# A transformer layer on one core: queries, keys and half the probabilities transposed by transfers, some low parts made by GpSimd, the head's loads placed anew

## The chip, the core and the metric

The kernel runs on one core of a Trainium2 chip. Time is the device time of one execution, in microseconds, as a median of several executions; the time before is 1294.08 us (three executions, 1293.95 to 1294.24). The profile is of one execution. Its engines are TensorE (PE, with PEld for its weight loads), VectorE (DVE), ScalarE (ACT), GpSimd (POOL) and SyncE (SP, which here only issues transfers).

## The reference, cut to what matters

One layer of a diffusion transformer is applied to two groups of 128 tokens: context ("prompt", s = 0 in the kernel) and latent ("sample", s = 1). Both use the same weights, all in float32.

```python
D_MODEL = 2048; HEAD_DIM = 128; A_HEADS = 8; A_KV_HEADS = 2; B_HEADS = 8; D_FF = 8192
def ada_mod(cvec, w_ada, b_ada):
    m = jax.nn.silu(cvec) @ w_ada + b_ada
    return jnp.split(m, 6, axis=-1)          # shift1, scale1, gate1, shift2, scale2, gate2
...
h = rms_norm(x, norm1_w) * (1 + sc1) + sh1
qa, ka, va, qb, kb, vb, ga, gb = project_heads(h, w_in, ...)    # one 2048 x 8704 product, then RMS norms on q and k
oa = window attention A (8 query heads, 2 key heads, a sink logit; rotary for latent tokens)
ob = neighbourhood attention B (8 heads, a position bias for latent tokens)
#    latent queries also see 128 cached context keys: two key blocks of 128; context queries see one block
ya = oa @ w_br_a;  yb = ob @ w_br_b
x = x + g1 * ((sigmoid(ga) * ya + sigmoid(gb) * yb) @ w_out)
h2 = rms_norm(x, norm2_w) * (1 + sc2) + sh2
x = x + g2 * (jnp.square(jax.nn.relu(h2 @ w_up)) @ w_down)
```

Beside the two token groups the outputs hold the context's keys and values.

## The kernel before, in words

**Products in three parts.** A float32 operand is split into a high part (rounded to the format that TensorE reads at full speed) and a low part, the rest. A product is three matmuls: high x high, low x high, high x low. Weights come from HBM as tiles of 128 partitions by 1024 columns (512 KB). ScalarE's copy writes the high part (`wH <- raw`, line 112), VectorE subtracts it to get the low part (`wL <- raw, wH`, line 277). For the weight tiles listed in `LO_DMA` the low part is made without VectorE: ScalarE writes minus the high part, and a transfer issued by GpSimd adds the weights to it from HBM (`minus_plus`).

**Steps.** The unit of the program's order is the step: one weight tile, 256 rows by 512 columns of a matrix, used for both token groups: 12 matmuls of 128 x 512. There are 456 steps: 0 to 71 for queries, keys and values, 72 to 135 for the gates, 136 to 167 for the two branches, 168 to 199 for `w_out`, 200 to 215 for the first up-projection columns, and from 216 on seven rounds of 16 steps of up-projection (`up_pair`, which forms two column blocks by fewer products of sums of weights, in the PSUM banks Q1 to Q7) and 16 of down-projection.

**What sets the order.** Each engine works through its instructions in the order in which the program issues them; `run()` walks over the steps and issues for each, in this order, loads that are due (`load_at`, table `RUN` says how far ahead), the high and low parts of coming steps (`prep_to`; `HIA` and `LOOK`), the step's matmuls, and the work hung on the step by `at(i, ...)` and `ex(i, ...)`. All places are tables of step numbers at the top of the file. Buffers come from fixed slots (table `SLOTS`): which slot each tile gets is written down, and a tile waits until its slot's last reader is done.

**The head.** The modulation for the first norm is made in two ways: pairs of 128-row blocks (`mod_pair`, eight loads `araw` of 512 KB and 64 small matmuls each, placed after the step in `ADA_AT`), and, for the last blocks, dot products by VectorE. `XS_AT` places the scaling of the activations.

**Dots.** The other modulation vectors (shift2, scale2, both gates) come from 288 instructions on VectorE, 128 rows x 1024 columns each: the transposed weights `aT` times the condition's row `cB`, summed along the row (line 1564). Both operands lie in SBUF; each load of `aT` serves two dots, one per token group. `DOTS1`, `DOTS` and `DOTS2` give the step of each load's pair.

**Attention.** `POST` gives the steps of the work on each of the seven query, key and value units `u`: `qk_stat` (sums of squares), `qk_apply` (norm and rotary), `qk_T`, in which TensorE transposes each head (128 x 128) into a PSUM bank `ps_qT`, from where ScalarE copies it out. `JOBS` gives the steps of eight attention jobs (mixer, token group s, half of the heads): scores, softmax, normalise, `probs_T` (TensorE transposes into `ps_PT`), values. Longer lists take another way, which the file has already and uses for the gates' merge and the MLP's activations: ScalarE writes two planes of 16-bit halves (`qk_planes`, `probs_planes`), SyncE's queue issues a transposing transfer (`qk_flip`, `probs_flip`), and ScalarE joins the halves again (`qk_join`, `probs_join`):

```python
fs = (qk_stat, qk_apply, qk_planes, qk_flip, qk_join) if len(ps) > 3 else (qk_stat, qk_apply, qk_T)
...
if flips:
    return scores, softmax, normalise, probs_planes, probs_flip, probs_join, values
return scores, softmax, normalise, probs_T, values
```

**PSUM** has eight banks of 128 x 512 float32: four accumulate the steps' products (`pacc`), four are for everything else (`paux`).

## Time and profile before

| | |
|---|---|
| median of three executions | 1294.08 us (1293.95 to 1294.24) |
| the profiled execution | 1294.03 us, of which the span of its instructions is 1291.9 us |
| DMA | 430.55 MB, 333 GB/s over the span |
| loads `raw <- in_w_in`, 512 KB each, issue to landing (median) | 9.9 us |
| accumulating transfers `wL <- in_w_down`, GpSimd's queue | 8.5 us |
| loads of the condition rows `cB <- silu` | 14, 512 KB each |

The page of the profile gives each engine's busy time as a share of the span, then the chain of work that ended last: followed back from the last instruction, it says on which engine the time lay that set the end. Rows of instruction groups read: line, engine, operation, output <- inputs, tile shape, count, then busy time and the mean length of one. A busy time of TensorE is modelled: matmuls overlap, so the distance between the starts of two instructions tells more than the length of one. Timeline rows begin with start and length in us.

### The profile page before, as it was taken

What the parts mean: (1) busy time and instruction counts of PE and PEld (TensorE: products, weight loads), DVE (VectorE), ACT (ScalarE), POOL (GpSimd) and SP (SyncE); (2) the same over time, 40 slices, a digit from 0 to 9 for tenths busy, and PEclk for the clock granted to TensorE, in tenths of its full rate; (3) what the DMA queues carried; (4) which work ended last, traced back from release to release, by engine and by line L of the source; (5) the groups of instructions that cost most, each with busy time, mean ns of one, the idle gap of its engine ahead of it and who ended that gap; (6) DMA issues with size and microseconds to landing.
All of it is one profiled execution on the core that took longest, in us unless ns stands there. A gap on an engine that the chain in (4) does not pass through costs nothing.

```text
span 1291.9 us, 18147 instructions
## 1 busy us (share of the span) xinstructions
PE 1281.9 (99%) x6082; PEld 1044.9 (81%) x6082; DVE 1209.6 (94%) x1611; ACT 960.6 (74%) x1363; POOL 105.9 (8%) x129
## 2 busy tenths in 40 slices
PE   8999999999999999999999999999999999999998
PEld 4777788888878888888887888888888888888887
DVE  4599999999999999999889999999999999999997
ACT  5535778888766765746798888888889887989871
POOL 0000002121200000001101000100000000010100
PEclk9999999999999999999999999999999999999999
DMA  9999999999999999998899999899898979979995
GB/s 377 418 420 418 380 385 387 329 351 327 369 360 354 385 383 330 364 392 259 265 279 329 295 329 307 273 350 313 272 355 249 321 267 311 344 231 361 385 341 166
DMA packets 158429, 430.55 MB, mean 333 GB/s; under 512 B 53072, under 2 KB 54336, under 8 KB 158336
## 3 DMA queue, kind: packets, MB, share of 16 engines
q1 hardware_dynamic: 145264, 383.39, 79.1%
q0 software_dynamic: 12880, 45.91, 16.6%
q8 instruction: 47, 0.77, 0.2%
q14 instruction: 46, 0.38, 0.1%
q10 hardware_dynamic: 192, 0.10, 0.1%
HBM read 403.35 MB, written 14.99 MB: 324 GB/s over the span
## 4 chain that ended last, share of the span: by engine, by line
PE 96%; DMA 3%; DVE 0%; ACT 0%; issue 0%; SPq 0%; ACTq 0%
PE acc L337 18%; PE acc L335 18%; PE acc L336 18%; PE Q L1338 7%; PE Q L1339 7%; PE Q L1337 7%; PE acc L466 5%; PE acc L468 5%; PE acc L467 5%; DMA raw<-in_w_in 2%; PE ps_ada L352 1%; PE ps_S L853 1%; DMA araw<-in_w_pair 1%; PE acc L1144 1%; PE acc L1143 1%; PE acc L1142 1%
## 5 line engine op out<-in xcount | busy, mean ns | idle before, releaser
L112 ACT ACTIVATE wH<-raw 128x1024 fp32r<-128x1024 f32 (+1 forms) x347 | 344.6, 1042 | 65.5 <-DMA raw<-in_w_in 18.6
L277 DVE TENSOR_TENSOR wL<-raw,wH 128x1024 fp32r<-128x1024 f32 x297 | 347.4, 1217 | 5.2 <-ACT wH L112 4.8
L1564 DVE CUSTOM_DVE_ANT_0 junk<-aT,cB,cols 128x1024 uint8<-128x1024 f32 x144 | 178.8, 1285 | 0.0
L466 PE MATMUL acc<-wH,hH 128*128 128x512 f32 x276 | 108.5, 393 | 0.0
L468 PE MATMUL acc<-wH,hL 128*128 128x512 f32 x276 | 107.5, 389 | 0.0
L467 PE MATMUL acc<-wL,hH 128*128 128x512 f32 x276 | 107.5, 389 | 0.0
L335 PE MATMUL acc<-wH,hH 128*128 128x512 f32 x256 | 102.9, 402 | 0.0
L337 PE MATMUL acc<-wH,hL 128*128 128x512 f32 x256 | 99.9, 390 | 0.0
L336 PE MATMUL acc<-wL,hH 128*128 128x512 f32 x256 | 99.8, 390 | 0.0
L1564 DVE CUSTOM_DVE_ANT_0 junk<-aT,cB,gc_g 128x1024 uint8<-128x1024 f32 x64 | 79.3, 1279 | 0.0
L112 ACT ACTIVATE uH<-raw 128x1024 fp32r<-128x1024 f32 x56 | 58.9, 1051 | 17.3 <-DVE raw L1409 15.4
L1415 DVE TENSOR_TENSOR tL<-t,tH 128x1024 fp32r<-128x1024 f32 x56 | 68.2, 1218 | 2.0 <-ACT tH L112 1.9
L1415 DVE TENSOR_TENSOR uL<-raw,uH 128x1024 fp32r<-128x1024 f32 x56 | 68.2, 1217 | 0.2
L1403 DVE TENSOR_TENSOR t<-raw 128x1024 f32<-128x1024 f32 x56 | 68.1, 1217 | 0.0
L112 ACT ACTIVATE tH<-t 128x1024 fp32r<-128x1024 f32 x56 | 58.7, 1049 | 9.5 <-DVE t L1403 7.3
L466 PEld LDWEIGHTS acc<-wH,hH 128*128 128x128 f32 x276 | 51.8, 188 | 12.5 <-issue 2.1
L468 PEld LDWEIGHTS acc<-wH,hL 128*128 128x128 f32 x276 | 51.8, 188 | 10.8
L467 PEld LDWEIGHTS acc<-wL,hH 128*128 128x128 f32 x276 | 51.9, 188 | 10.6
L112 ACT ACTIVATE XH<-raw 128x1024 fp32r<-128x1024 f32 x56 | 58.6, 1047 | 0.5 <-PE Q L1338 0.5
L337 PEld LDWEIGHTS acc<-wH,hL 128*128 128x128 f32 x256 | 48.0, 188 | 10.2
L335 PEld LDWEIGHTS acc<-wH,hH 128*128 128x128 f32 x256 | 48.1, 188 | 10.0 <-issue 0.7
L336 PEld LDWEIGHTS acc<-wL,hH 128*128 128x128 f32 x256 | 48.2, 188 | 9.9 <-issue 0.7
(673 smaller groups left out, 3389.4 us busy)
## 6 DMA issues: line engine op xcount, KB each, us to landing
raw<-in_w_in SPq DMA_DIRECT2D x133, 512.0 KB, 9.9
raw<-in_w_down SPq DMA_DIRECT2D x128, 512.0 KB, 9.3
raw<-in_w_upF SPq DMA_DIRECT2D x112, 512.0 KB, 6.3
aT<-in_w_adaT SPq DMA_DIRECT2D x80, 512.0 KB, 9.8
aT<-in_w_gT SPq DMA_DIRECT2D x64, 512.0 KB, 9.9
araw<-in_w_pair SPq DMA_DIRECT2D x48, 512.0 KB, 9.9
raw<-in_w_out SPq DMA_DIRECT2D x32, 512.0 KB, 9.7
XL<-in_w_upF POOLq DMA_DIRECT2D x21, 512.0 KB, 8.1
```

The lines of the kernel that those rows point to most:

```text
L112: act.activation(out, in_, AF.Copy)
L277: dve.tensor_tensor(st["lo"], st["raw"], st["hi"].bitcast(F32), op=OP.subtract)
L335: pe.matmul(acc[tb], sh, wh[:, k, :], start=f, stop=False, **kw)
L336: pe.matmul(acc[tb], sh, wl[:, k, :], start=False, stop=False, **kw)
L337: pe.matmul(acc[tb], sl, wh[:, k, :], start=False, stop=l, **kw)
L466: pe.matmul(acc[tb], sh, wh[:, k, :], start=kt == 0 and k == 0 and not held and not seeded, stop=False, **kw)
L467: pe.matmul(acc[tb], sh, wl[:, k, :], start=False, stop=False, **kw)
L468: pe.matmul(acc[tb], sl, wh[:, k, :], start=False, stop=last and k == 1 and not hold, **kw)
L1337: pe.matmul(acc, stat[0], hi, start=f, stop=False)
L1338: pe.matmul(acc, stat[0], lo, start=False, stop=False)
L1415: dve.tensor_tensor(b[n + "L"], v, b[n + "H"].bitcast(F32), op=OP.subtract)
L1564: dve.tensor_tensor_reduce(out, box["raw"], cB[s, tag], 1.0, dst if second else baT[:, part, fb:fb + 1], OP.mult, OP.add, dst)
```

## The change

- **Transposes.** All seven lists of `POST` get five entries, and the four jobs on latent tokens (s = 1, two key blocks) seven: their transposes go by planes, transposing transfer and join. The four jobs on context tokens keep TensorE's. For query units of mixer A the join also applies the scale that the copy out of PSUM applied.
- **PSUM.** `paux` has two banks instead of four; a new pool `pwide` holds one tile of two banks, used in turn by the modulation of the very first blocks, by a copy of a condition row (`cW`), and by the banks Q4 and Q3 of `up_pair`. The product Q3 of a round's last block moves ahead in the order, so that Q5 ends last.
- **Dots.** ScalarE copies a condition row into the two-bank PSUM tile (`cond_up`, as many steps ahead of the dots as the table `CW` says), and dots read it there, except the 42 pairs listed in `BUF`, which read SBUF as before. Dots are grouped two loads at a time (`dot_runs`): two dots with one row, then two with the other.
- **Low parts by GpSimd.** `POOL_LO` names for 79 such pairs of dots a step whose low part GpSimd is to subtract at the same time (`lo_pool`), if it has none by then; VectorE writes one column of it just before, which orders the slot's reuse.
- **Tables.** `LO_DMA` falls from 65 entries to 39. The second to sixth modulation pairs, the scalings, the constants, the dots and the sums of the MLP get new steps; `HIA`, `LOOK`, `RUN` and `SLOTS` are new throughout.

```diff
-DOTS1 = [16, 17, 17, 19, 21, 27, 28, 32, 33, 34, 34, 38, 38, 38, 40, 40]
+DOTS1 = [15, 22, 24, 25, 29, 30, 31, 33, 34, 35, 36, 38, 40, 40, 42, 42]
...
-LO_DMA = [54, 64, 77, 81, 90, 96, 98, 104, 106, 107, 113, 115, 125, 126, 134, 137, 147, 154, 167, 179, 193, 195, 197, 199, 202, 203, 215, 216, 220, 222, 224, 226, 228, 230, 235, 242, 248, 252, 271, 277, 280, 294, 297, 302, 312, 316, 328, 335, 340, 346, 354, 356, 370, 382, 386, 390, 393, 397, 403, 408, 418, 434, 438, 448, 449]
+LO_DMA = [79, 130, 169, 182, 186, 199, 210, 220, 222, 230, 239, 241, 248, 252, 254, 279, 286, 290, 311, 312, 324, 342, 352, 354, 356, 362, 374, 378, 382, 386, 390, 403, 406, 407, 414, 418, 422, 436, 451]
...
-ADA_AT = [None, 5, 13, 20, 24, 38]
-XS_AT = {1: 14, 2: 2, 3: 23}
-POST = {('kvA', 0): [54, 57, 78], ('qA', 0): [54, 59, 66], ('qA', 1): [62, 70, 79], ('kB', 0): [71, 71, 79], ('qB', 0): [75, 82, 91], ('kB', 1): [89, 101, 104], ('qB', 1): [82, 87, 106]}
-JOBS = [[81, 85, 87, 93, 102], [82, 84, 88, 97, 111], [80, 86, 97, 103, 112], [88, 98, 103, 109, 111], [103, 103, 106, 115, 122], [105, 105, 108, 109, 126], [108, 108, 119, 123, 126], [113, 114, 117, 121, 125]]
+ADA_AT = [None, 4, 10, 19, 24, 39]
+XS_AT = {1: 0, 2: 10, 3: 26}
+POST = {('kvA', 0): [56, 58, 72, 75, 76], ('qA', 0): [52, 58, 68, 69, 74], ('qA', 1): [57, 65, 70, 83, 83], ('kB', 0): [74, 77, 81, 85, 90], ('qB', 0): [70, 73, 90, 93, 95], ('kB', 1): [80, 95, 105, 106, 109], ('qB', 1): [80, 83, 88, 93, 95]}
+JOBS = [[80, 81, 86, 102, 113], [86, 87, 97, 99, 102, 103, 108], [90, 90, 92, 108, 125], [95, 96, 104, 107, 113, 113, 118], [100, 100, 115, 119, 123], [106, 106, 109, 114, 120, 124, 128], [115, 115, 119, 123, 125], [117, 117, 119, 122, 124, 126, 128]]
...
+RN = 2
+BUF = [0, 2, 9, 12, 15, 16, 21, 24, 29, 31, 32, 34, 38, 40, 45, 47, 50, 52, 55, 60, 62, 65, 66, 69, 71, 73, 76, 82, 84, 94, 97, 100, 102, 104, 108, 117, 123, 127, 133, 135, 139, 143]
...
+POOL_LO = {43: 89, 44: 94, 46: 95, 48: 100, 49: 101, 51: 102, 57: 109, 58: 110, 59: 111, 61: 112, 88: 153, 116: 246, 118: 269, 119: 272, 120: 276, 122: 278, 124: 307, 125: 308, 128: 334, 129: 337, 130: 336, 141: 402, 53: 103, 68: 125, 86: 150, 41: 88, 126: 310, 89: 152, 4: 31, 132: 346, 72: 128, 87: 157, 54: 106, 121: 277, 90: 154, 93: 158, 134: 369, 80: 136, 96: 168, 138: 376, 91: 155, 8: 39, 98: 171, 22: 58, 14: 45, 33: 80, 115: 247, 81: 144, 77: 133, 5: 35, 64: 119, 3: 30, 136: 371, 83: 143, 19: 55, 42: 92, 7: 42, 109: 185, 28: 70, 137: 373, 10: 41, 111: 196, 27: 68, 103: 172, 70: 126, 107: 195, 23: 61, 67: 120, 79: 139, 142: 404, 101: 173, 99: 170, 114: 242, 105: 184, 17: 50, 110: 183, 78: 132, 92: 162, 36: 82}
...
-    paux = ctx.enter_context(tc.tile_pool(name="paux", bufs=4, space=bass.MemoryType.PSUM))
+    paux = ctx.enter_context(tc.tile_pool(name="paux", bufs=2, space=bass.MemoryType.PSUM))
+    pwide = ctx.enter_context(tc.tile_pool(name="pwide", bufs=1, space=bass.MemoryType.PSUM))
...
+    def lo_pool(st):
+        if "lo" in st or "hl" in st:
+            return
+        pool_hi(st)
...
+        st["lo"] = G("wL", F32R)
+        pool_minus(st["lo"], st["raw"], st["hi"])
+
+    def pool_minus(lo, full, hi):
+        dve.tensor_copy(lo[:, 0:1], hi.bitcast(F32)[:, 0:1])
+        pool.tensor_tensor(lo, full, hi.bitcast(F32), op=OP.subtract)
...
-        for s, w in enumerate({"qB": (2, 2), "kB": (None, 3)}.get(u[0], ())):
+        for s, w in enumerate({"qA": (0, None), "qB": (2, 2), "kB": (None, 3)}.get(u[0], ())):
...
-            for name in ("Q3", "Q4", "Q5") + (("Z",) if len(fast) < 8 else ()):
+            box["Q4"], box["Q3"] = pair("Q43")
+            for name in ("Q5",) + (("Z",) if len(fast) < 8 else ()):
...
-                    todo.append(("Q3", sc(j, 3), b["XH"][:, hi], b["XL"][:, hi]))
+                    todo.insert(4 if end else 5, ("Q3", sc(j, 3), b["XH"][:, hi], b["XL"][:, hi]))
...
+    def cond_up(s, q, tag):
+        cW[0] = wide("cW")
+        copy(cW[0], cB[s, tag])
+
+    def dots_of(k, run_, s, q, tag):
+        if k in POOL_LO:
+            lo_pool(wsteps[POOL_LO[k]])
+        for box, job, later in run_:
+            dot(box, job, later, s, cB[s, tag] if k in BUF else cW[0])
+        if k + 1 in POOL_LO:
+            pool_hi(wsteps[POOL_LO[k + 1]])
```

Three places show what the tables move. The first is TensorE's order at the end of the first units, where `ps_qT` receives the transposed heads of `u_qA` and `u_kB`; before:

```order
L335 MATMUL acc<-wH,hH_1663 128x512
L336 MATMUL acc<-wL,hH_1663 128x512
L337 MATMUL acc<-wH,hL_1664 128x512
L782 MATMUL ps_qT<-ident,u_qA_1862 128x128 x8
L782 MATMUL ps_qT<-ident,u_kB_2233 128x128 x8
L335 MATMUL acc<-wH,hH_244 128x512
L336 MATMUL acc<-wL,hH_244 128x512
```

and after, at the same place:

```order
L374 MATMUL acc<-wL,hH_1733 128x512
L375 MATMUL acc<-wH,hL_1734 128x512
L373 MATMUL acc<-wH,hH_246 128x512
L374 MATMUL acc<-wL,hH_246 128x512
L375 MATMUL acc<-wH,hL_247 128x512
```

The matmuls of one unit's last step are followed directly by those of the next unit's first, with no transposes between.

The second is SyncE's order of loads in the head (`raw` weights of the steps, `araw` the modulation pairs, `cB` the condition rows, `aT` weights for dots); before:

```order
L531 DMA raw<-in_w_in 128x512 x3
L243 DMA raw<-in_w_in 128x1024 x6
L344 DMA araw<-in_w_pair 128x1024 x8
L243 DMA raw<-in_w_in 128x1024 x7
L1545 DMA cB_442<-silu 128x1024
L1545 DMA cB_444<-silu 128x1024
L243 DMA raw<-in_w_in 128x1024
L344 DMA araw<-in_w_pair 128x1024 x8
```

and after:

```order
L569 DMA raw<-in_w_in 128x512 x3
L256 DMA raw<-in_w_in 128x1024 x5
L382 DMA araw<-in_w_pair 128x1024 x8
L256 DMA raw<-in_w_in 128x1024 x6
L382 DMA araw<-in_w_pair 128x1024 x8
L256 DMA raw<-in_w_in 128x1024
L1593 DMA cB_423<-silu 128x1024
L1593 DMA cB_425<-silu 128x1024
```

Five weight loads instead of six stand ahead of the second modulation pair, and the third pair stands ahead of the condition rows instead of behind them.

The third is VectorE's order in the stretch of the dots beside attention (`cB` a condition row in SBUF, `cW` its copy in PSUM); before:

```order
L1564 ISA junk,shT_159<-aT,cB_1210,cols 128x1024
L1564 ISA shT_159 128x1
L277 TENSOR_TENSOR wL<-raw,wH 128x1024 x2
L1564 ISA junk,shT_159<-aT,cB_1212,cols 128x1024
L1564 ISA shT_159 128x1
L277 TENSOR_TENSOR wL<-raw,wH 128x1024
```

and after:

```order
L1612 ISA junk,shT_162<-aT,cW,cols 128x1024
L1612 ISA shT_162 128x1
L1612 ISA junk,scT_163<-aT,cW,cols 128x1024
L1612 ISA scT_163 128x1
L330 CAST wL<-wH 128x1
L1612 ISA junk,shT_162<-aT,cW,cols 128x1024
L1612 ISA shT_162 128x1
L1612 ISA junk,scT_163<-aT,cW,cols 128x1024
L1612 ISA scT_163 128x1
L290 TENSOR_TENSOR wL<-raw,wH 128x1024
```

Two dots of one row now stand together, they read `cW`, and a one-column cast stands ahead of a pair beside which GpSimd makes a low part.

More of the change, by code (lines that the diff above doesn't have):

```diff
@@ L106, in SM, with wide, pair @@
         return slot(sp, "s", [P, 8], F32, name)[:, :n]
+    def wide(name):
+        return pwide.tile([P, 1024], F32, name=name, tag="w")
+    def pair(name):
+        t = wide(name)
+        return t[:, 0:512], t[:, 512:1024]
     def bank(name, pool_=None):
@@ L348, in pair_mm_q @@
         if j == 0 and q == 0:
-            box["ps"] = bank("ps_ada")
+            box["ps"], box["sel"] = pair("ps_ada") if alone else (bank("ps_ada"), None)
         raw = box.pop((fb, q)).rearrange("p (k n) -> p k n", k=4)
@@ L390, in first_cols @@
         shT, scT = mod[0]
-        ps = bank("ps_sel")
+        ps = box.pop("sel")
         for i in (1, 0):
@@ L1551, in dot_load, with dot @@
         sync.dma_start(box["raw"], src)
-    def dot(box, job, second, s, tag):
+    def dot(box, job, second, s, row):
         which, fb = job
@@ L1563, in dot @@
         out = sp.tile([P, 1024], mybir.dt.uint8, name="junk", tag="J", bufs=2)
-        dve.tensor_tensor_reduce(out, box["raw"], cB[s, tag], 1.0, dst if second else baT[:, part, fb:fb + 1],
+        dve.tensor_tensor_reduce(out, box["raw"], row, 1.0, dst if second else baT[:, part, fb:fb + 1],
                                  OP.mult, OP.add, dst)
@@ L1617, in dots2 @@
+    def dots2():
+        order = [(("g2", fb), q, q) for q in range(2) for fb in range(KC)]
+        at_, n0 = list(DOTS2), 0
+        for r, n in enumerate(RUNS2):
+            dot_runs(at_[n0:n0 + n], order[n0:n0 + n], ("g", r), 2)
+            n0 += n
         for n in range(4):
-            i = DOTS2[(15, 15, 23, 31)[n]] + ROW_AT[n]
+            i = DOTS2[31] + ROW_AT[n]
             while wsteps[i]["key"][0] != "down":
```

121 lines of the change are left out of this document (74 added, 47 removed).

## The prediction

> **What bounds the kernel now.** I read the page first (busy times, the chain of waits by engine), then the chain in order of time, then timelines of single places.
>
> ```profile
> span 1291.9 us, 18147 instructions
> PE 1281.9 (99%) x6082; PEld 1044.9 (81%) x6082; DVE 1209.6 (94%) x1611; ACT 960.6 (74%) x1363; POOL 105.9 (8%) x129
> PEclk9999999999999999999999999999999999999999
> PE 96%; DMA 3%; DVE 0%; ACT 0%; issue 0%; SPq 0%; ACTq 0%
> ```
>
> TensorE's work is the time: 96% of the chain that ended last lies on it, at the full granted clock, and the 3% of DMA lie in the head. A busy TensorE alone would prove little, since matmuls overlap; the chain decides. So an instruction taken off TensorE is worth its pitch, and any other engine's work is worth nothing until it makes TensorE wait. VectorE, at 94%, is the nearest to that. The sum below is made on the profiled execution, 1294.03 us, of which 1291.9 are the span; the runs' median is 1294.08, so nothing is to be converted.
>
> **1. Transposes leave TensorE.** The trace has 52 transposes of queries and keys and 48 of probabilities:
>
> ```profile
> L782 PE MATMUL ps_qT<-ident,u_qA x16: 270/272/273, 226.7 to 264.2; 128*128 128x128 f32 x16
> L782 PE MATMUL ps_qT<-ident,u_kB x16: 272/272/273, 264.3 to 344.0; 128*128 128x128 f32 x16
> L782 PE MATMUL ps_qT<-ident,u_qB x16: 270/272/273, 303.3 to 352.1; 128*128 128x128 f32 x16
> L782 PE MATMUL ps_qT<-ident,u_kvA x4: 270/272/273, 260.2 to 260.5; 128*128 128x128 f32 x4
> L900 PE MATMUL ps_PT<-ident,prob x48: 270/272/273, 309.6 to 409.9; 128*128 128x128 f32 x48
> ...
> 262.97 0.39 PE L336 MATMUL acc<-wL,hH 128*128 128x512 f32 x1
> 263.20 0.40 PE L337 MATMUL acc<-wH,hL 128*128 128x512 f32 x1
> 263.44 1.04 PE L782 MATMUL ps_qT<-ident,u_qA 128*128 128x128 f32 x8
> 264.31 1.04 PE L782 MATMUL ps_qT<-ident,u_kB 128*128 128x128 f32 x8
> 265.10 0.48 PE L335 MATMUL acc<-wH,hH 128*128 128x512 f32 x1
> 265.42 0.40 PE L336 MATMUL acc<-wL,hH 128*128 128x512 f32 x1
> ```
>
> All 52 go, and the 32 of the four jobs with two key blocks; 16 stay. One lasts 272 ns, but they overlap: from 263.44 to 265.42 stand 16 transposes and one matmul (0.23 us, from 262.97 to 263.20), so 16 cost 1.98 - 0.23 = 1.75 us, or 0.109 us each, with the change-over included. 84 x 0.109 = **-9.2 us**. Nothing else leaves or joins TensorE.
> The Trainium skill (TensorE: Matmul & The Clock Gate, Part 4: PE-mode transpose) gives about 275 ns for a transpose in a kernel's context; by that the term would be -23 us. The trace shows that length too, 272 ns, but as a length that overlaps its neighbour's, and the row decides.
>
> **2. The head.** The loads of the second modulation pair now stand one load earlier in SyncE's queue, and TensorE takes the pair one step earlier (after step 4, not 5).
>
> ```profile
> 20.93 2.17 SPq L243 DMA_DIRECT2D raw<-in_w_in  x3
> 23.40 8.46 SPq L344 DMA_DIRECT2D araw<-in_w_pair  x8
> 32.82 7.78 SPq L243 DMA_DIRECT2D raw<-in_w_in  x7
> ...
> 38.12 3.23 PE L352 MATMUL ps_ada<-araw,early 128*32 128x256 f32 x56
> 42.06 0.64 PE L352 MATMUL ps_ada<-araw,early 128*32 128x256 f32 x8 [0.71 <-DMA araw<-in_w_pair]
> 42.63 0.50 PE L466 MATMUL acc<-wH,hH 128*128 128x512 f32 x1
> ```
>
> Eight issues take 9.42 us, 1.18 each: the queue moves at the pace of the transfers. The pair's last transfer now lands 1.2 us sooner, so TensorE leaves the pair at 41.4 instead of 42.63; but step 5 (12 matmuls x 0.23 = 2.7 us) then still lies ahead of it, where before it was done: **+1.5 us**. Ends: 0, if the queue is quicker there, and +2.7, if the pair's last load gains nothing. The later pairs move by as much in the loads as in the steps and have no stall in the chain, so they cost nothing.
>
> **3. Low parts by GpSimd beside dots that read PSUM.** The table holds 79, but 15 of its steps already have a low part when their turn comes: in the program's order GpSimd makes 64. VectorE loses 38 subtractions and gains 64 one-column casts; 27 accumulating transfers and ScalarE's 26 negations for them go; ScalarE gains 40 copies of the condition rows into PSUM. No row shows a GpSimd subtraction of 128x1024.
>
> ```profile
> 286.69 0.69 DVE L872 TENSOR_REDUCE mx<-ps_S 128x4 f32<-128x512 f32 x1
> 286.85 0.56 POOL L717 TENSOR_SCALAR_AFFINE_SELECT bias<-bias 64x384 f32<-64x384 f32 x1
> ...
> 335.06 1.28 DVE L1564 CUSTOM_DVE_ANT_0 junk<-aT,cB,cols 128x1024 uint8<-128x1024 f32 x1
> 336.26 1.56 DVE L1564 CUSTOM_DVE_ANT_0 junk<-aT,cB,cols 128x1024 uint8<-128x1024 f32 x1
> 336.82 1.42 POOL L719 TENSOR_SCALAR_AFFINE_SELECT bias<-bias 64x384 f32<-64x384 f32 x1
> ...
> L187 POOL TENSOR_TENSOR early<-early 32x128 f32<-32x128 f32 x1 | 0.4, 448 | 7.8 <-ACT early L186 7.8
> ...
> 195.50 3.49 DVE L277 TENSOR_TENSOR wL<-raw,wH 128x1024 fp32r<-128x1024 f32 x3
> 198.91 1.28 DVE L1564 CUSTOM_DVE_ANT_0 junk<-aT,cB,cols 128x1024 uint8<-128x1024 f32 x1
> ...
> L1109 DVE TENSOR_TENSOR t<-g,acc 128x512 f32<-128x512 f32 x15 | 10.2, 680 | 3.9 <-PE acc L1272 2.9 <-PE acc L1144 0.6 <-PE acc L337 0.4
> L1110 DVE TENSOR_TENSOR x<-x,t 128x512 f32<-128x512 f32 x8 | 5.5, 692 | 0.3
> ```
>
> These rows show a collision: the select takes 0.56 us beside a reduction that reads PSUM, and 1.42 beside a dot with both operands in SBUF, and that dot 1.56 instead of 1.28. A dot that reads PSUM should leave GpSimd alone, and should last as long as now (680 against 692 ns where one operand is PSUM). Two dots cover 2 x 1.20 = 2.4 us (335.06 to 336.26). GpSimd's subtraction lies between 0.56 x 1024/384 = 1.5 us (one input) and 8 x 0.448 = 3.6 us (two inputs, small, fixed cost counted eight times); I take the middle, 2.5. It overruns the two dots by 0.2 us at most, which VectorE pays only where a two-operand subtraction follows. VectorE: -38 x 1.14 (195.50 to 198.91 for three) + 64 x 0.1 = -37 us, with 64 x 0.2 = 13 of overrun still -24. It is not on the chain, so this buys little: the one place where TensorE waits for it after the head is
>
> ```profile
> 704.19 0.50 PE L1337 MATMUL Q<-uH,h22H 128*128 128x512 f32 x1
> 705.45 0.50 PE L1338 MATMUL Q<-uL,h22H 128*128 128x512 f32 x1 [0.76 <-DVE uL L1415]
> ```
>
> where 1.26 - 0.23 = 1.0 us is to be had; I take half, **-0.5**, between 0 and -1.0.
> The Trainium skill (SBUF — State Buffer, Who interferes with whom) says that a VectorE instruction with two SBUF inputs and a GpSimd instruction that reads SBUF lock each other out for the whole instruction, and not with one SBUF input; the 1.56 and 1.42 agree. The skill (GPSIMD Engine Reference, Performance versus the Vector engine) gives 4497 ns for a subtraction's like of 2048 elements; half of it, an estimate, is 2.2 us, inside the dots' cover.
>
> **4. What the transfers cost elsewhere.** In place of TensorE's transposes, ScalarE writes planes of half-words, SyncE's queue transposes them, and ScalarE joins them.
>
> ```profile
> 215.00:415.00 200.00, 200.00 (x975) 166.38 (x974) 197.05 (x304) 154.39 (x360) 31.59 (x29) 1.00 0.99 350
> ...
> L112 ACT ACTIVATE fTa<-pTa 128x1024 uint16<-128x1024 uint16 x32 | 41.9, 1362 | 7.6 <-DMA pTa<-pla 7.6
> L112 ACT ACTIVATE pla<-up 128x1024 uint16<-128x1024 uint16 x32 | 32.5, 1047 | 1.2 <-PE acc L336 0.7 <-PE acc L337 0.3
> L112 ACT ACTIVATE acc<-dsum 128x512 f32<-128x512 f32 x44 | 24.9, 591 | 5.6 <-DVE t L1109 3.0 <-DVE dsum L1491 2.6
> L283 ACT ACTIVATE wL<-wH 128x1024 fp32r<-128x1024 f32 x44 | 46.5, 1060 | 1.0
> ...
> ACT fTm L112 <- DMA pTm<-plm: 12.0, 3, 6.2
> ...
> ACT fTa L112 <- DMA pTa<-pla: 7.6, 2, 7.3
> ```
>
> From 215 to 415 us (window view: after the pair of times, busy PE, PEld, VectorE 197.05, ScalarE 154.39, GpSimd) ScalarE gets: 12 planes at 1.05 and 18 short ones at 0.6 (23 us), 21 half joins at 1.36 (29), 8 scalings at 0.6 (5), 8 copies into PSUM at 2 x 0.59 (9), and loses 12 negations at 1.06, 8 probability and 14 query and key evacuations at 0.6 (26 in all). Net +40, so 194 of 200 us. TensorE has its next high parts several steps (of 2.7 us) ahead, which covers short waits at the joins. I take **+0.5 us**, between 0 and +8 (three steps of delay).
> The transfers' own load balances: 11 transposes come, 14 accumulating transfers of that stretch go.
>
> **Sum:** 1294.0 - 9.2 + 1.5 - 0.5 + 0.5 = **1286.3 us**, 0.6% less. Its own terms' ends give 1284 to 1295.
>
> **Rivals.**
> *ScalarE waits for the transfers (slower).* Place: the joins between 215 and 415 us. All three transposes of the merged rows waited, 12.0 us in all, 4.0 each; of the MLP's activations' transposes only two did (7.6). Against it: most joins stand some steps behind their transfer. For it: the first join of one query tile stands at its transfer's own step, and ScalarE has 6 us of slack where VectorE had 3. At 4.0 each, 11 waits are 44 us: 194 + 44 - 200 = 38 late, of which some 7 steps of work ahead, 19 us, hide half: 1286.3 + 19 = **1305**. It decides from 25 us of waiting (2.3 per join), and makes the kernel slower than before from 33 (3.0).
> *GpSimd collides with VectorE (slower).* If its subtraction takes 3.6 us, it overruns the dots by 1.2; the 64 casts and overruns then cost 64 x 1.3 = 83 us against 43 saved, most of it in the stretch that had 3 us of VectorE free: there 20 low parts x 1.3 - 8 x 1.14 = 17 us over, less 3: 1286.3 + 14 = **1300**. It decides from 2.4 + 0.4 us a piece.
> *The order also heals the head.* If the new places cost nothing there and the 1.0 us is won whole: 1294.0 - 10.2 - 1.4 (the stall of 42.06 and the 0.71 before it) = **1282**.
> *The transposes were hidden anyway:* 1294. Against it: TensorE issues matmuls right before and behind them, with no gap.
>
> **Chances.** Forecast 0.70, ScalarE's waits 0.12, the collision 0.10, the healed head 0.05, hidden 0.03. The likeliest gives **1286.3**. The range is 1282 to 1297: below it 0.05, above it the full sizes of the two slower rivals, 0.13. What this measurement can't tell from no change is 0.2%, 2.6 us. The forecast and the healed head, 0.75, and 0.02 of half-sized rivals are faster: 0.77. Half-sized rivals and the hidden case are the same: 0.10. Slower: 0.13.
>
> **What would show it.** Right: 84 transposes fewer at an unchanged pitch of 0.109; dots on the PSUM rows at about 1.28 us; GpSimd's subtraction at 2 to 2.8 us; TensorE leaving the second pair near 41.4 with step 5 still to come; ScalarE at 95% or more from 215 to 400 us. Wrong: TensorE waiting for high parts behind joins, or for low parts while GpSimd runs; dots or subtractions of VectorE stretched beside GpSimd.

## The result and the profile after

The changed kernel takes 1309.82 us (median of four executions, 1307.53 to 1312.74) against 1294.06 (1293.95 to 1294.24). That is 1.0123 times the time before, with an interval of 1.0100 to 1.0145: slower by 15.8 us, where 1286.3 had been forecast. The profiled execution took 1307.53 us, of which 1305.8 are the span.

The page of the changed kernel has this, in the places of the rows shown of before; in the last two rows the number behind the busy time is the mean of one in ns:

```profile
span 1305.8 us, 18166 instructions
PE 1279.1 (98%) x5998; PEld 1038.2 (80%) x5998; DVE 1172.3 (90%) x1637; ACT 1009.9 (77%) x1404; POOL 231.4 (18%) x167
PEclk9999999999999899999999999999999999999999
PE 58%; DMA 5%; DVE 5%; ACT 3%; issue 3%; POOL 0%; DVEq 0%; SPq 0%; ACTq 0%; POOLq 0%
...
L331 POOL TENSOR_TENSOR wL<-raw,wH 128x1024 fp32r<-128x1024 f32 x62 | 149.3, 2408 | 546.5 <-DVE wL L330 287.2
L1612 DVE CUSTOM_DVE_ANT_0 junk<-aT,cW,cols 128x1024 uint8<-128x1024 f32 x102 | 126.1, 1273 | 2.5 <-ACT cW L125 2.5
```

Read alone, the first rows say that the change worked. There are 84 matmuls fewer, VectorE lost the 37 us that were forecast, GpSimd's subtraction takes 2.41 us and a dot on the PSUM rows 1.27. The chain is less help than before. Read back from the last instruction it reaches only to 337.23 us, where it lies on VectorE, so its 58% for TensorE can't be set beside the 96% of before; the kernel without one transfer that is shown below has 62% and is not slower than the one before. But the longest pieces of the chain are now transfers far behind the head, and one slice of the granted clock is an 8.

Where the time went is best seen from the starts of the steps' matmuls of 128 x 512 (those that write `acc` and `Q`), of which both kernels have the same number, 5298. The k-th of one is set beside the k-th of the other (us from the span's start):

```
  k      before    after    difference   since the row above
  300    107.51    107.98     +0.47         +0.47     (the head)
  900    249.33    248.91     -0.42         -0.89
 1400    387.83    375.87    -11.96        -11.54
 1500    412.81    404.30     -8.51         +3.45     (transposes gone)
 1600    439.97    442.56     +2.59        +11.10     <- here
 2100    554.36    558.26     +3.90         +1.31
 2800    718.55    725.68     +7.13         +3.23
 3100    786.69    795.14     +8.45         +1.32
 3500    877.41    890.29    +12.88         +4.43
 5200   1263.24   1277.27    +14.03         +1.15
```

Up to 404 us nearly all went as forecast. Then 11.1 us are lost between two rows, and some 11 more in small pieces behind. Of the 11.1, 1.1 are lost in the same place by the kernel without the transfer that is to blame: at the row of 1500 the changed kernel still has two matmuls of the values ahead (`ps_o` of `u_kvA`, 407.02 to 407.88 us) that the kernel before has behind it:

```profile
407.02 1.02 PE L962 MATMUL ps_o<-probT,u_kvA 128*128 128x512 f32 x2
407.88 1.05 PE L966 MATMUL ps_o<-probT,u_vB 128*128 128x128 f32 x8
```

The waits of TensorE in the changed kernel from 300 us on (the waiting and the releasing instruction; us in total, times, the longest) and the windows of that place (columns as in the window view of before):

```profile
PE ps_o L966 <- ACT probT L125: 8.0, 1, 8.0
PE Q L1376 <- DVE tL L1462: 5.1, 3, 3.2
PE acc L373 <- ACT up L125: 1.4, 1, 1.4
PE Q L1376 <- DMA XL<-in_w_upF: 0.8, 2, 0.4
```

```profile
215.00:415.00 200.00, 199.59 (x931) 164.32 (x930) 193.72 (x310) 186.03 (x370) 59.93 (x35) 1.00 1.04 346
418.00:427.00 9.00, 1.03 (x10) 0.84 (x8) 2.04 (x3) 2.66 (x2) 0.00 (x0) 0.85 1.09 198
427.00:431.00 4.00, 4.00 (x18) 3.90 (x19) 0.69 (x1) 1.53 (x4) 0.00 (x0) 0.50 1.02 414
```

One wait of 8 us stands at 418 us, where the engines do next to nothing while the DMA engines read as fully busy (1.09) and move 198 GB/s, where 346 is the rule. Behind it TensorE works for 4 us at a granted clock of 0.50, which costs 2 us more: together the other 10.0 of the 11.1. The chain in order of time shows its first piece and what the wait was for (start, length, what), and the timelines of ScalarE, SyncE and GpSimd show the pieces:

```profile
337.23 1.20 DVE junk L1612
...
394.72 9.31 DMA pTP<-plP
404.12 2.42 POOL wL L331
406.56 17.70 DMA pTP<-plP
424.34 2.49 ACT probT L125
426.87 3.78 PE ps_o L966 x16
```

```profile
406.48 0.91 POOL L297 DMA_DIRECT2D wL<-in_w_in  x1
...
406.56 5.72 SPq L951 DMA_TRANSPOSE pTP<-plP  x1
...
415.36 1.03 ACT L125 ACTIVATE cW<-cB 128x1024 f32<-128x1024 f32 x1 [3.96 <-DVE gc_g L1612]
424.34 2.48 ACT L125 ACTIVATE probT<-pTP 128x2048 uint16<-128x2048 uint16 x1 [7.95 <-DMA pTP<-plP]
```

The last job's transposing transfer of the probabilities (`plP`, 512 KB in 2048 packets of 256 bytes) took 17.7 us from issue to landing; the one before it took 9.3 (the chain's row of 394.72), and the tile view has 5.5 as the shortest of the four. 0.08 us ahead of it GpSimd had issued one of the accumulating transfers that stay in `LO_DMA` (step 130). The packets of that time, for each us the number and mean length of the transposing ones (256 bytes) and the accumulating ones (4096 bytes):

```
   us     256 B: n, ns    accumulating: n, ns    all, GB/s
  407        0                  0                  447
  411      323,  25             1,  513            300
  412      373,  52            26, 1368            218
  413        7, 260             7,  436             30
  414       16, 198            18,  327             78
  416      251,  56            12,  707            113
  418      112,  83             9,  549             66
  420      123, 103             8,  327             64
  422       51, 348             2,  327             21
  423      360,  19             0                  285
```

Once the last accumulating packet is gone the transposing packets take 19 ns again. Between 412 and 423 us the two crawl beside each other and nothing else moves: the loads that SyncE had queued behind the transposing transfer wait with them.

### The profile page after: what moved, and what is told of

Same layout as the page of the kernel before. It is cut to its first block, busy times and chain, and to the rows that moved or that the text cites. A ratio compares the mean times of both kernels' runs of the same rounds, so it can differ in the third digit from the quotient of the medians.

```text
span 1305.8 us, 18166 instructions
## 1 busy us (share of the span) xinstructions
PE 1279.1 (98%) x5998; PEld 1038.2 (80%) x5998; DVE 1172.3 (90%) x1637; ACT 1009.9 (77%) x1404; POOL 231.4 (18%) x167
## 4 chain that ended last, share of the span: by engine, by line
PE 58%; DMA 5%; DVE 5%; ACT 3%; issue 3%; POOL 0%; DVEq 0%; SPq 0%; ACTq 0%; POOLq 0%
PE acc L373 13%; PE acc L375 13%; PE acc L374 13%; PE Q L1376 5%; PE Q L1377 5%; PE Q L1375 5%; DMA pTP<-plP 2%; DMA pTa<-pla 1%; DMA XL<-in_w_upF 1%; DVE junk L1612 1%; DMA raw<-in_w_down 1%; ACT wH L125 1%; DVE uL L1462 1%; PE acc L1182 1%; PE acc L1199 1%
## 5 line engine op out<-in xcount | busy, mean ns | idle before, releaser
L290 DVE TENSOR_TENSOR wL<-raw,wH 128x1024 fp32r<-128x1024 f32 x260 | 306.6, 1224 | 20.0 <-ACT wH L125 19.5
L331 POOL TENSOR_TENSOR wL<-raw,wH 128x1024 fp32r<-128x1024 f32 x62 | 149.3, 2408 | 546.5 <-DVE wL L330 287.2
L1612 DVE CUSTOM_DVE_ANT_0 junk<-aT,cW,cols 128x1024 uint8<-128x1024 f32 x102 | 126.1, 1273 | 2.5 <-ACT cW L125 2.5
L125 ACT ACTIVATE uH<-raw 128x1024 fp32r<-128x1024 f32 x56 | 58.8, 1050 | 11.9 <-DVE raw L1456 6.2
L125 ACT ACTIVATE cW<-cB 128x1024 f32<-128x1024 f32 x40 | 40.8, 1021 | 33.6 <-DVE scT L1612 18.1
L504 PEld LDWEIGHTS acc<-wH,hH 128*128 128x128 f32 x276 | 51.8, 188 | 12.6 <-issue 1.6
L505 PEld LDWEIGHTS acc<-wL,hH 128*128 128x128 f32 x276 | 51.8, 188 | 10.4
L1612 DVE CUSTOM_DVE_ANT_0 junk<-aT,cW,gc_g 128x1024 uint8<-128x1024 f32 x44 | 54.3, 1271 | 2.4 <-ACT cW L125 2.4
```

The source lines that it names most:

```text
L125: act.activation(out, in_, AF.Copy)
L290: dve.tensor_tensor(st["lo"], st["raw"], st["hi"].bitcast(F32), op=OP.subtract)
L331: pool.tensor_tensor(lo, full, hi.bitcast(F32), op=OP.subtract)
L504: pe.matmul(acc[tb], sh, wh[:, k, :], start=kt == 0 and k == 0 and not held and not seeded, stop=False, **kw)
L505: pe.matmul(acc[tb], sh, wl[:, k, :], start=False, stop=False, **kw)
L1612: dve.tensor_tensor_reduce(out, box["raw"], row, 1.0, dst if second else baT[:, part, fb:fb + 1], OP.mult, OP.add, dst)
```

## The experiments

Two theories stood at the start. **A:** a transposing transfer that meets an accumulating one crawls, and the step 130 meeting makes most of the loss. **B:** VectorE is late everywhere because of the dots that the tables moved out of the tail into the rounds, and the wait at 418 us is only the first sign of it. A third, **C**, came up on the way: the join stands too few steps behind its transfer, whatever the transfer does. The kernel before was timed again beside each group of runs and took 1294.07 to 1294.23 us, so that times of different groups may be compared.

### The two transfers by themselves

No layer is computed here, only transfers in cases that follow one another, four times each:

```diff
+    def case(c, flip, accs, loads, plain=0):
+        ...
+            for x in los:                     # accumulating, GpSimd's queue
+                pool.dma_start(x, src(), accum_op=OP.add)
+            for x in gs:                      # plain, GpSimd's queue
+                pool.dma_start(x, src())
+            for x in raws:                    # plain, SyncE's queue
+                sync.dma_start(x, src())
+            if flip:
+                sync.dma_start_transpose(pT, pl)
+    case("A", True, 0, 0); case("B", False, 1, 0); case("C", True, 1, 0); case("D", True, 2, 0)
+    case("E", True, 0, 4); case("F", True, 1, 4); case("G", False, 1, 4); case("H", True, 0, 0, 1)
```

> No layer is computed: only transfers of 512 KB in eight cases, four times each, one after another. A: a transposing transfer alone. B: an accumulating transfer alone. C: both together. D: one transposing and two accumulating. E: four loads, then the transposing transfer, on SyncE's queue. F: E with an accumulating transfer beside it. G: one accumulating transfer and four loads. H: a transposing transfer beside a plain load on GpSimd's queue. Theory A: A lands in 3.6 to 4 us, C in 10 to 18 us, D in more, E in 7 to 9, F in 12 to 20, G in 7 to 9, H in 4 to 6 (it is the accumulating, not the queue). If bandwidth alone were shared: C 5 to 6, D 7 to 8, F 9 to 10 us.

The tile view of this probe gives the landings: the transposing transfer alone (A), the accumulating one alone (B), both together (C, in the two rows behind):

```profile
L73 SPq DMA_TRANSPOSE pTA<-plA x4: 1424/1799/1922, 4.3 to 18.6; - x4
DMA to landing us min/median/max: 4.2/4.3/4.3
...
L67 POOL DMA_DIRECT2D loB<-in_w_down x4: 857/868/1022, 25.6 to 43.7; - x4
DMA to landing us min/median/max: 5.1/5.3/5.3
...
L73 SPq DMA_TRANSPOSE pTC<-plC x4: 1317/1977/2084, 51.4 to 82.3; - x4
DMA to landing us min/median/max: 8.2/8.4/11.6
```

Together they take 8.4 us, nearly the sum of 4.3 and 5.3, as if one had run behind the other, and once 11.6. With a plain load by GpSimd in the accumulating one's place (H) it is 6.3. So they do collide, but by half of what the kernel shows, and less than the 10 to 18 us that theory A expected: this alone did not carry it.

### Gate-2 dots left out

The 64 dots of the second gate are replaced by copies of one column:

```diff
+        if which == "g2" and GATE2_OUT:
+            dve.tensor_copy(g2col[fb // 4][:, s, fb % 4:fb % 4 + 1], box["raw"][:, 0:1])
+            return
```

> The 64 dots of the second gate (VectorE, steps 233 to 400) are left out, a one-column copy stands for each; the transfers stay as they are. It takes some 73 us of work off VectorE between 700 and 1110 us. Theory A: the waits near 418 (11 us with the slow clock) and 699 stay, those near 790 and 857 to 884 shrink only as far as VectorE had a share in them: 1304 to 1308. Theory B: the waits of TensorE between 780 and 1214 us go, 1300 to 1303.

1307.82 us, ratio 1.0107 (1.0092 to 1.0122): 2 us less than the changed kernel and within what theory A expected, though the dots left out last 81 us together (64 x 1.27) and VectorE's busy time on the page fell from 1172.3 to 1116.7 us. The wait of TensorE for the last join is as long as before, since the transfer is (tile view of `pTP`; who waited, and its landings):

```profile
  PE ps_o L967: 9.0, 1
DMA to landing us min/median/max: 5.9/8.8/18.7
```

Theory B fails its first test.

### One low part, ten low parts: first attempt

Step 130's low part is made by a subtraction on GpSimd instead of minus the high part and the accumulating transfer; in the second kernel that of nine more steps whose transfer meets a transposing one.

```diff
+NO_ACC = [130]            # second kernel: [130, 220, 222, 252, 254, 286, 290, 386, 414, 418]
-    def minus_plus(lo, hi, src):
+    def minus_plus(lo, hi, src, full=None):
+        if full is not None:
+            pool.tensor_tensor(lo, full, hi.bitcast(F32), op=OP.subtract)
+            return
```

> The low part of step 130, which an accumulating transfer makes just as the last transposing transfer of the probabilities starts, is made by GpSimd's subtraction instead. Theory A (a transposing transfer that meets an accumulating one crawls): the transposing transfer issued near 406 us lands within 10 us instead of 17.7, TensorE's wait of 8.1 us near 418 and the 3 us of half clock behind it go, the kernel takes 1299 us (1296 to 1302). Theory B (VectorE is overfull between 560 and 1214 us because dots were moved there from the tail): nothing lost lies near 418, 1307 to 1312. Theory C (two steps between transfer and join are too few, whatever else moves): a wait of 2 to 5 us stays, 1302 to 1306.

> As the run before, and nine more accumulating transfers that were under way with a transposing transfer (steps 220, 222, 252, 254, 286, 290, 386, 414, 418) are replaced by GpSimd subtractions. Theory A: all transposing transfers behind 400 us land within 11 us, the waits near 699, 790 and 857 to 884 us shrink from 10.5 us to 2, the kernel takes 1291 us (1288 to 1294). Theory B: the GpSimd subtractions take VectorE's port where it is overfull already, nothing is won behind 640 us: 1299 to 1303.

1340.18 (1.0358, 1.0341 to 1.0375) and 1352.81 us (1.0455, 1.0439 to 1.0471). Neither tells anything of the theories. A subtraction holds its weight tile longer than a transfer does, so the table `SLOTS` had to be made anew, and 131 tiles got other buffers. In the first kernel the wait at 418 us fell to 2.2 us, and by 437 us it was 5.2 us ahead of the changed one; then loads came late all over the rest, since their buffers came free late (TensorE's wait for `tH`, `dsum` and `g_gB`, 8.9 us the longest). What this shows is the price of the buffer table: the same edit with the old table, next, is 46 us faster.

### One low part, with the buffers kept

The same edit, with the old table except that two buffers trade their names from step 130 on.

> The edit of e1, with the buffers kept: two buffers change names from the place of the edit on, no tile waits for another owner than before (in e1, 131 tiles had other buffers, and behind 490 us loads came late). Theory A: 6 to 11 us less than the changed kernel, 1299 to 1304. Theory B: no gain, 1307 to 1312. If the loss of e1 behind 490 us came from the edit and not from the buffers: 1335 or more.

1293.93 us (1291.99 to 1299.41), ratio 1.0005 (0.9995 to 1.0015): **15.9 us less than the changed kernel, by one transfer**, and more than the 6 to 11 us that theory A expected. The landing of the four transposing transfers is 5.3 to 9.1 us. 2.3 us of TensorE's waiting stay at 418 us with another cause, which ScalarE's timeline shows: the transfer has landed at 415.3, but the join stands behind a copy of a condition row that waits for VectorE's dots.

```profile
413.99 0.58 ACT L126 ACTIVATE oHB<-ps_o 128x512 fp32r<-128x512 f32 x1
417.84 1.03 ACT L126 ACTIVATE cW<-cB 128x1024 f32<-128x1024 f32 x1 [3.27 <-DVE gc_g L1616]
418.80 2.46 ACT L126 ACTIVATE probT<-pTP 128x2048 uint16<-128x2048 uint16 x1
```

### Eleven low parts, with the buffers kept

> As e1b, and ten more accumulating transfers that were under way with a transposing one (steps 220, 222, 252, 254, 279, 286, 290, 386, 414, 418) replaced by GpSimd subtractions; buffers change names at two places. Theory A: the waits near 699 and 855 to 884 shrink too (from 8 us to 2): 1293 to 1297. Theory B: GpSimd's subtractions lengthen VectorE's two-operand subtractions between 640 and 1200 us, where VectorE has no slack: 1300 to 1310, and behind 640 us nothing is won.

1315.67 us, ratio 1.0164 (1.0147 to 1.0181): slower than one low part by 21.7 us and outside both expectations, though the eleven meetings are gone and no transposing transfer behind 400 us is longer than 11.0. What changed shows in the page's group of GpSimd's subtractions in the rounds:

```profile
L298 POOL TENSOR_TENSOR XL<-raw,XH 128x1024 fp32r<-128x1024 f32 x9 | 52.3, 5807 | 56.6 <-ACT XH L126 41.3
```

and in the timelines of GpSimd and VectorE at one of them:

```profile
664.02 8.16 POOL L298 TENSOR_TENSOR XL<-raw,XH 128x1024 fp32r<-128x1024 f32 x1 [6.75 <-ACT XH L126]
...
668.64 0.68 DVE L1456 TENSOR_TENSOR YB<-raw,YB 128x512 fp32r<-128x512 f32 x1
669.24 0.68 DVE L1457 TENSOR_TENSOR raw<-t,raw 128x512 f32<-128x512 f32 x1
669.96 2.78 DVE L1460 TENSOR_TENSOR raw<-raw 128x512 f32<-128x512 f32 x1
```

There VectorE has two-operand instructions from SBUF, no dots from PSUM. GpSimd's subtraction, 2.41 us beside the dots, takes 5.81 in the mean. By these rows it stands still while VectorE's run (VectorE is busy for 8.12 of its 8.16 us), and when it gets its turn, VectorE's next one stands still instead (2.78 us for 0.68). By the view of waits TensorE then waits for VectorE's low parts `tL`, 15.0 us in twelve waits. This is the mechanism of the second rival of the prediction, real, but not in the place where the change put GpSimd's work. The Trainium skill (SBUF — State Buffer, Who interferes with whom) says that a VectorE instruction with two SBUF inputs contends with a GpSimd instruction that reads SBUF, by an exclusive lock, and that one with at most one SBUF input does not. Both halves of the rule agree with these rows and the 1.27 us of the dots.

### The probabilities' transposes back on TensorE

```diff
-JOBS = [..., [86, 87, 97, 99, 102, 103, 108], ..., [117, 117, 119, 122, 124, 126, 128]]
+JOBS = [..., [86, 87, 97, 103, 108], ..., [117, 117, 119, 126, 128]]
```

and so for all four jobs on latent tokens, with TensorE's transposes at the steps of the joins.

> The four jobs on latent tokens have five steps again: their 32 transposes go back to TensorE at the place of the join, and the four transposing transfers of the probabilities go. Theory A: no meeting near 406 us, the wait of 8.1 us and the slow clock go, 32 x 0.109 = 3.5 us come: 1301 to 1304. If the lateness near 418 us is ScalarE's (its joins and planes), it goes as well, but the accumulating transfer of step 130 then changes nothing in e1b; both runs together tell. Theory B: 1311 to 1315.

1320.72 us, ratio 1.0209 (1.0193 to 1.0224). TensorE waits 7.3 us in four places for the copies that free the PSUM bank of its transposes, and 9.2 us later for low parts; buffers had to be reassigned as well. The time lies outside both expectations. The 8-us wait is gone, but what is in its place comes from where I put the transposes. So the run decides nothing.

### The 64 low parts on VectorE

```diff
-        pool_minus(st["lo"], st["raw"], st["hi"])
+        dve.tensor_tensor(st["lo"], st["raw"], st["hi"].bitcast(F32), op=OP.subtract)
```

> The 64 low parts that GpSimd makes are made by VectorE at the same place in its order, the one-column casts go. VectorE gets 64 x (1.14 - 0.07) = 68 us. If GpSimd's help is worth what it frees, TensorE loses where VectorE has no slack (43 to 400 us and 560 to 1214 us): 1325 to 1365. If the loss of the changed kernel is GpSimd's doing (its subtraction of 2.4 us against VectorE), the kernel gets faster: below 1307.

1349.36 us, ratio 1.0424 (1.0403 to 1.0446): **39.5 us more than the changed kernel**. VectorE has 1236.1 us of work, and TensorE waits for it: 14.1 us at `tL` alone. With 26 accumulating transfers fewer, and its tables as they are, the kernel cannot do without it.

### The full overlap by itself

The probe again, eight times each, with plain loads ahead of the transposing transfer, as in the kernel, so that its packets begin when the accumulating ones are well under way:

```diff
+    case("A", True, 1, 1); case("B", True, 1, 2); case("C", True, 1, 3); case("D", True, 0, 2)
+    case("E", True, 0, 2, 1); case("F", True, 2, 2); case("G", True, 2, 0); case("H", True, 0, 3)
```

> Only transfers again, eight cases, eight times each; now one to three loads stand ahead of the transposing transfer on SyncE's queue, so that it starts later, when the accumulating transfer's data are on the way. A, B, C: one, two, three loads, then the transposing transfer, an accumulating one beside them. D: two loads and the transposing one, no accumulating. E: as B with a plain load on GpSimd's queue instead of the accumulating. F: two accumulating, two loads. G: two accumulating, no load. H: three loads, no accumulating. Theory A (full overlap is what crawls): A, B or C has transposing transfers of 15 us and more from issue to landing where D has 6 to 7 and E 8; the times of one case spread by several us. If the 17.7 us of the changed kernel came from elsewhere: none over 12 us.

The tile view of this probe, one load, transposing and accumulating (A), and two loads without the accumulating transfer (D):

```profile
L73 SPq DMA_TRANSPOSE pTA<-plA x8: 3391/6249/6875, 5.7 to 83.9; - x8
DMA to landing us min/median/max: 8.7/9.5/15.7
...
L73 SPq DMA_TRANSPOSE pTD<-plD x8: 4183/4322/4546, 284.6 to 338.9; - x8
DMA to landing us min/median/max: 6.2/6.4/6.6
```

Here the crawl of the kernel is to be had outside it. Of eight equal cases of A, two crawl: their last packets come 15.2 and 12.1 us after the issue, those of the six others after 8.2 to 9.4. With two loads ahead and the accumulating transfer it is 9.3 to 9.6, without it 6.2 to 6.6, and with a plain GpSimd load in its place 7.5 to 8.0. Nothing crawled without an accumulating transfer in the game, and with one, two of eight equal cases did, at some 25 to 160 GB/s. The packets show one difference. In the two that crawl all 128 packets of the accumulating transfer start between the first and the last of the transposing one, in the six others 102 to 112 of them. In the crawl at 406 us of the changed kernel it is all 128, too. With the plain load by GpSimd (H of the first probe) all 128 start inside as well, and nothing crawls. But it is no rule: in the MLP of the changed kernel a transposing transfer has its last packet after 14.7 us (issued at 850 us) with 50 such packets inside. Why some pairs crawl stays open.

### The join one step earlier

One low part by GpSimd as above, and the last job's join at step 125 instead of 126, ahead of the copy that it stood behind:

```diff
-[117, 117, 119, 122, 124, 126, 128]
+[117, 117, 119, 122, 124, 125, 128]
```

> e1b, and the last job's join one step earlier (125 instead of 126), so that on ScalarE it stands ahead of the copy of a condition row into PSUM, which waits for VectorE's dots until 417.8 us while the transfer has landed at 415.3. Theory A with the queue: TensorE's wait of 2.5 us near 419 us goes: 1291.5 (1290 to 1293.5). If the wait is the transfer's: 1293 to 1295.

1292.05 us (1290.45 to 1295.06), ratio 0.9986 (0.9976 to 0.9995). The wait at 418 us is gone whole: theory C is worth about 2 us, and only once the transfer is quick (in the changed kernel the copy is done at 416.4 us, and the join waits for the transfer alone until 424.3). This is the one kernel with all its work that is faster than both, by 0.14% (some 2 us) against the one before and by 17.8 us against the changed one.

### Three accumulating transfers more

If meetings are the cause, more of them should bring the loss back. The last kernel, with steps 216, 228 and 244 added to `LO_DMA`:

> e10, and three low parts of the MLP (steps 216, 228, 244) by accumulating transfers instead of VectorE's subtractions: VectorE has 3.4 us less to do between 640 and 780 us, where TensorE waits for it three times (691, 697, 780 us, 3.2 us in e1b). Theory B for what is left: 1289 to 1291. Theory A: two of them lie near transposing transfers and may meet them: 1293 to 1299, with a wide spread.

1303.50 us (1301.87 to 1310.08), ratio 1.0069 (1.0052 to 1.0086): 11.5 us more, above both expectations. The tile view of the MLP's transposing transfers:

```profile
L1037 SPq DMA_TRANSPOSE pTa<-pla x16: 1570/3564/10999, 665.8 to 1248.2; - x16
DMA to landing us min/median/max: 3.7/6.0/20.9
```

One transposing transfer, 13.9 us in the last kernel, now takes 20.9, beside an accumulating one, for whose like (`XL`) TensorE waits 3.6 us, 0 in the kernel without the three. But this does not show that three more meetings cost 11.5 us. The two accumulating transfers beside it are in the last kernel as well, at the same distance; the three new ones are issued at 648, 698 and 728 us, it at 848. And the buffer table had to change, too, in 78 of its entries. The run agrees with theory A and does not prove it; it shows again that equal meetings cost unequal times.

### One low part, gate-2 dots left out

The second test of theory B, now without the meeting of step 130:

> e1b without the 64 dots of the second gate (left out, one-column copies in their place; 73 us less on VectorE between 540 and 1110 us). Theory B (what is left of the loss is VectorE's load from the dots that moved there): the waits near 691, 697, 780, 1112 and 1122 us go, 1288 to 1290. If what is left has another cause: 1292 to 1294.

1293.58 us, ratio 1.0004 (0.9993 to 1.0014), against 1.0005 with the dots. The waits near 697 and 780 us go, those near 693, 1112 and 1122 stay, and the time is the same, though VectorE has 55 us less to do (1173.8 and 1118.6 busy): theory B falls.

### One, eleven and eleven other transfers left out

The cleanest test of theory A changes no buffer and no other instruction of the changed kernel. Only the accumulating transfers of the listed steps are not issued: that of step 130; the eleven that meet a transposing one; and eleven that meet none, as a control.

```diff
+OUT = [130]   # second: [130, 220, 222, 252, 254, 279, 286, 290, 386, 414, 418]
+              # third: [182, 186, 199, 210, 248, 311, 312, 342, 354, 362, 403]
+        if i not in OUT:
             pool.dma_start(lo, src.bitcast(F32R), accum_op=OP.add)
```

> The changed kernel, and the accumulating transfer of step 130 is left out (its low part stays minus the high part); nothing else, no buffer and no other instruction moves. Theory A: as e1b, 1292 to 1297. If e1b's gain came from its two buffers or from GpSimd's subtraction: 1306 or more.

> The eleven accumulating transfers that meet transposing ones (steps 130, 220, 222, 252, 254, 279, 286, 290, 386, 414, 418) are left out. Theory A: the waits near 418, 699 and 857 to 884 go, and with the meetings the spread of the runs: 1287 to 1291, within 2 us. If the meetings behind 640 us cost nothing: as e13.

> The control: eleven accumulating transfers that meet no transposing one (steps 182, 186, 199, 210, 248, 311, 312, 342, 354, 362, 403) are left out. Theory A: no gain, 1305 to 1311. If it is the number of accumulating transfers or their bytes (5.8 MB, 1.4%) that costs: as e14.

| left out | us (range) | ratio to before | less than the changed kernel |
|---|---|---|---|
| step 130's | 1292.57 (1291.20 to 1294.78) | 0.9989 (0.9980 to 0.9998) | 17.2 |
| eleven that meet | 1290.99 (1289.64 to 1292.45) | 0.9976 (0.9966 to 0.9987) | 18.8 |
| eleven that don't | 1304.21 (1300.83 to 1306.66) | 1.0077 (1.0056 to 1.0097) | 5.6 |

The tile view of the probabilities' transposing transfers says why, first with step 130's transfer left out, then of the control:

```profile
L953 SPq DMA_TRANSPOSE pTP<-plP x4: 3724/5958/7135, 333.5 to 406.7; - x4
DMA to landing us min/median/max: 5.7/8.7/9.2
```

```profile
  ACT probT L126: 5.8, 1
DMA to landing us min/median/max: 4.7/8.0/15.5
```

One transfer of 512 KB, left out, gives back the whole loss: **theory A stands**. The eleven that meet nothing give a third of it, just below the 1305 us that theory A expected at least; the crawl stays, somewhat shorter (15.5 us for 17.7, and 5.8 us of TensorE's wait for 8.0). So fewer transfers have a worth of their own, but not this one. Two things are beyond the 10.0 us of the place itself. With step 130's transfer left out the waits between 857 and 884 us are gone too, and the MLP's first transposing transfer, whose last packet came after 13.5 us in the changed kernel, has it after 7.2: the stretch behind runs at another offset, and transfers meet otherwise. And the times of the changed kernel spread by 5.2 us, those of before by 0.3. With the eleven meetings gone they still spread by 2.8, so that the meetings are at most a part of this; the rest is not explained.

## Why the prediction was wrong, point by point

- **What bounds the kernel** was read rightly, TensorE, and so was what an instruction taken off it is worth.
- **Step 1, the transposes, -9.2 us.** Right in the mechanism, and 1 us too large. The kernel is ahead of the one before by 8.5 us at 404 us, with 0.5 lost in the head, but 0.9 of this are the two matmuls of the values that are still to come there: 8.1. In the kernel without step 130's transfer, at the row of 1600, where both have all of attention behind them, it is 7.2 + 0.6 = 7.9. The sum by lengths of 272 ns, -23 us, is refuted by the same rows.
- **Step 2, the head, +1.5.** +0.5 was measured, inside its ends of 0 and +2.7. TensorE leaves the second pair at 40.66 us instead of the 41.4 that I had worked out: the pair's last load gained 2.0 us, not 1.2. Of these 1.4 come from its eight issues, which ended at 30.46 us instead of 31.86, and 0.6 from the load, which landed 9.9 us behind its issue instead of 10.5.
- **Step 3, GpSimd.** The sizes were right: 2.41 us for 2.5, dots at 1.27 for 1.28 on the PSUM rows, casts 145 ns for 0.1 to 0.2, VectorE -37 us. (The accumulating transfers that go are 26, not 27.) The half microsecond was not won: in the stretch where the kernel before waits 0.8 us for VectorE, near 705 us, the changed one waits 3.2, and 1.3 are left with the eleven meetings gone. That the same low parts cost 39.5 us on VectorE says that the kernel now needs GpSimd, not what the step gained. And the mean of -37 us hid where VectorE lost work. The windows of before:

```profile
900.00:1110.00 210.00, 210.00 (x928) 173.74 (x927) 202.31 (x231) 177.95 (x204) 13.89 (x18) 1.00 0.91 296
1200.00:1292.00 92.00, 87.43 (x392) 72.10 (x390) 83.95 (x115) 55.37 (x66) 9.05 (x14) 0.99 0.87 290
```

and after:

```profile
900.00:1110.00 210.00, 209.91 (x927) 173.18 (x926) 209.20 (x260) 180.46 (x213) 39.01 (x30) 1.00 0.94 309
1214.00:1306.00 92.00, 87.33 (x392) 71.87 (x390) 50.66 (x56) 53.83 (x66) 7.72 (x13) 0.99 0.59 202
```

  The 33 us came out of the tail, where VectorE had time anyway. In the rounds it has 209.2 of 210 us instead of 202.3. Even with all eleven meetings gone, at 1290.99, the kernel misses the forecast by 4.7 us: it is 7.2 us ahead at 433 us, with all of attention behind it, and 3.1 at 1260, lost in five pieces of 0.5 to 1.4. TensorE's waits for low parts from 400 us on are 2.6 us of that (`tL` 1.8, `m2L` 0.6, `wL` 0.2). That the second gate's dots are not their main cause is shown (above); what in the order of ScalarE and VectorE is, stays open.
- **Step 4, the transfers, +0.5. This is the step that failed**, with its last sentence: "The transfers' own load balances: 11 transposes come, 14 accumulating transfers of that stretch go." I counted load, and that roughly: from 215 to 415 us the trace of before has 12 accumulating transfers, that of the changed kernel 2. What decided was who meets whom: one accumulating transfer that stayed is issued 0.08 us ahead of a transposing one that came, and the two together take 17.7 us, where without it all four land after 9.2 at most. That is 10.0 us in its place and 17.2 in all. The order of GpSimd's and SyncE's issues might have shown that the two lie close. Its price no row of before could have told. Transposing and accumulating transfers were in flight together there too (at 477 us, last packet after 11.9 us behind 630 packets of loads), but of an accumulating weight's 128 packets never more than 20 start between the first and last packet of a transposing transfer, and none crawled. ScalarE's own work I had put at 194 of 200 us; it was 186.
- **The rival "ScalarE waits for the transfers", 1305,** named the place, the joins between 215 and 415 us and just behind, and the sign, and came within 5 us, but for a wrong reason. It priced eleven waits of 4.0 us, from the waits at the merged rows. Up to 415 us there was none over 0.2: the joins stood far enough behind. One wait of 8.0 came behind, from a collision of transfers, which no rival had. Its 0.12 was too little, since I gave the unknown of step 4 one mechanism only.
- **The rival of the collision of GpSimd and VectorE, 1300,** did not come true in the change, and did when I moved low parts to where VectorE has two operands in SBUF (21.7 us for ten).
- **The range,** 1282 to 1297, was built from the sum's terms and half-sized rivals, and so left out that one late transfer stops all engines at once.

## What to carry to other kernels

When a change adds transposing transfers, look up at every place which accumulating transfer is in flight then, by the two queues' orders, and move or drop the accumulating one, or put the consumer further behind than a crawl lasts (17.7 us here; no run tried this); counting bytes or transfers does not find this. Where a join or a copy waits, ask first what stands ahead of it on its engine, since with the transfer mended the next cause was a copy ahead of it. And read a saved total of an engine by stages: 33 us saved where the engine had time were worth nothing here, and an edit may move work into a stage that had none to spare.

## What the runs showed of the hardware that I had not expected

- A transposing transfer of 512 KB and an accumulating one, 4.3 and 5.3 us alone, take 8.4 us together, and in some cases up to 15.7 in the probe and 20.9 in a kernel. In the changed kernel's crawl the DMA engines move 20 to 120 GB/s and all read as busy, and packets of 256 bytes take 50 to 350 ns instead of 19. With one or two plain loads instead, the same transposing transfer takes 5.7 to 7.2.
- What queues behind such a pair on SyncE waits as well: no load's packet started between 412 and 423 us.
- Behind 8.0 us without work TensorE had half its clock for 4 us (0.50 in the window from 427 to 431 us), so that the wait cost 10, not 8. The Trainium skill (TensorE: Matmul & The Clock Gate, Part 1) has such a half-rate state after an idle window; the trace agrees.
